# Attention's q and k kept in scratch as four rows a channel, so that one DMA of 128 rows loads an operand

## The chip, the cores and the metric

The kernel runs on one core of one Trainium2 chip. The metric is the device time of one execution in microseconds (us). The engines are PE (matrix multiply, TensorE), DVE (VectorE), ACT (ScalarE), POOL (GpSimd) and SP (SyncE, which here only issues DMAs). A profile comes from one execution, with the start and length of every instruction.

## What is computed

Two layers of a backbone over 1024 latent and 256 context tokens (T = 1280 columns, 1024 channels). A layer is: norm, one projection into four groups of heads (gated DeltaNet, Hyena, HGRN2, differential attention), an output projection, and an MLP. The part that the change touches is the differential attention, cut to what matters:

```
q = rope(rms_norm(q)); k = rope(rms_norm(k))     # 4 heads, two halves j of 32 channels
s = einsum('bqhjd,bkhjd->bhjqk', q, k) * scale
pr = softmax(s)
w = pr[:, :, 0] - lam * pr[:, :, 1]
o = einsum('bhqk,bkhe->bqhe', w, v)
```

Everything is float32. The products of q and k run on PE in the format F32R: each operand is split into a rounded part (hi) and the rest (lo), and one matmul over 128 rows adds up four products of 32 rows each. For that q stands in SBUF as the rows hi, lo, hi, lo and k as hi, hi, lo, lo, 32 rows each.

## The kernel before, in words

A layer runs in stages, each a Python generator; `mix` and `weave` interleave two of them by weights, and a scheduler of the framework then sets the order on each engine within what depends on what. Engines work through their own queue in order. SP has one queue for nearly all loads and stores: a DMA that waits, or whose descriptors find no room, holds up all that stand behind it.

The stages around the change, in `run` (L1723):

- `project` (L448) makes the projections, a unit of 128 channels at a time. What follows a unit is done in chunks of 512, 512 and 256 tokens; for q and k it is `post_d` (L637): inverse norm, rope, then `split` into the one buffer `dhl` (tag `lf`, one buffer, shared with HGRN2's `lf`). ACT copies the hi part (L254), DVE subtracts to get the lo part (L255), and SP stores both with one DMA (L657).
- `scratch` (L427) lays out the buffers in DRAM. `dq` and `dk` are `[2, 128, 2, T]`: hi or lo, channel, block of 128 channels, token. So a channel has one row of 5 KB for hi and one for lo, far apart.
- `hgrn` (L988) runs as the leading stage, and `rest()` in `run` as the filling one: the end of `project`, then the loads of attention's first head (`load` in `attn`, L1146), then `hyena` (L1441) woven with the modulation products `mods` (loads `modw`, L341; matmuls `pmod`, L363).
- `attn` (L1137) then leads, with what is left of `hyena`, `mods` and the next layer's filters as the fill. Each of its four heads needs two q tiles and two k tiles of 128 rows. The loads of the next head are issued when the third query block of a head begins (`qi == 2`).

`load` fills a tile with two DMAs, each of 64 rows. For q the source is hi and lo of 32 channels, the same both times. For k it is hi of 32 channels repeated twice, then lo repeated twice, a source with a step of zero in its outermost dimension. So a head is 8 DMAs, and both layers together have 64.

`hyena` transposes its input on PE first (`put`, L1468). The input `u` is loaded at L1455, and the filter bases (`bfl`, `bil`, `bfc`, `bic`) at L1311, gates (`xg`) at L1458. In layer 0 it runs for the context tokens first and then for the latents, in one and the same buffer `u`: the first pass stores its result (L1542) before the second pass loads. In layer 1 it runs for the latents only.

Of the kernel before, what the change touches and what calls it, by code (L numbers as in the profile page):

```python
# [9 lines left out]
F32 = mybir.dt.float32  # L10
# [11 lines left out]
T = SEQ + CTX  # L22
# [218 lines left out]
class K:  # L241
# [185 lines left out]
    def scratch(self, l):  # L427
        S = self.S = {}
        for n in CM_COL:
            if n in ("hf", "hb"):  # L430
                S["k" + n] = self.dram(f"k{n}_{l}", [128, 2, T])
                S["l" + n] = self.dram(f"l{n}_{l}", [128, T // 64, 2, 2, 64])
            elif n in ("dq", "dk"):
                S[n] = self.dram(f"{n}_{l}", [2, 128, 2, T])
            elif n[0] != "g":
                S[n] = self.dram(f"{n}_{l}", [128, 2, T])
        g = self.dram(f"g_{l}", [128, 6, T])
        S["gk"], S["gv"], S["gq"] = [g[:, 2 * j:2 * j + 2] for j in range(3)]
        for n in list(S):
            for i in range(2):  # L440
                S[n, i] = S[n][:, :, i] if n in ("lhf", "lhb", "dq", "dk") else S[n][:, i]
        S["g"] = g
        for n, a, w in TM:
            S[n] = self.dram(f"{n}_{l}", [128, NT, w])
        for k in range(KT):
            S["o", k] = self.dram(f"o{k}_{l}", [128, T])
# [190 lines left out]
    def post_d(self, l, tp, name, i, u, a, n):  # L637
        nc = self.nc
        u = u[:, a:a + n]
        r = self.inv_norm(tp, u, self.c["bones32"], 1.0 / 32, 32 * EPS)  # L640
        y = self.e(tp, 2, n)
        nw = self.P["dqw" if name == "dq" else "dkw"]
        nc.vector.scalar_tensor_tensor(y, u, nw, r, ALU.mult, ALU.mult)
        if a < SEQ:

            rc, rs = self.e(tp, 1, n), self.e(tp, 3, n)
            nc.sync.dma_start(rc, self.i["c_rcos"][:, a:a + n])
            nc.sync.dma_start(rs, self.i["c_rsin"][:, a:a + n])
            t2 = self.e(tp, 0, n)
            p = self.aux("prope")  # L650
            nc.tensor.matmul(p[:, :n], self.c["rperm"], y, start=True, stop=True)
            nc.vector.tensor_mul(t2, p[:, :n], rs)
            nc.vector.tensor_mul(y, y, rc)
            nc.vector.tensor_add(y, y, t2)
        hl = tp.tile([128, 2, 512], F32R, tag="lf", name="dhl", bufs=1)
        self.split(hl[:, 0, :n], hl[:, 1, :n], y, lo_eng=nc.vector)
        nc.sync.dma_start(self.S[name, i][:, :, a:a + n].rearrange("x p t -> p x t"), hl[:, :, :n].bitcast(F32))  # L657


    def gdn(self, l):  # L660
# [476 lines left out]
    def attn(self, l, qp):  # L1137

        nc, tc, S, P = self.nc, self.tc, self.S, self.P
# [6 lines left out]
        def load(i, b):  # L1146

            out = ops[i, b] = []
            for j in range(2):
                r = slice(64 * b + 32 * j, 64 * b + 32 * j + 32)  # L1150
                for nm, n in (("q", 128 * NQ), ("k", T)):
                    t = pools[heads.index((i, b)) % 2].tile([128, T], F32R, tag=f"{nm}{j}", name=f"{nm}{j}")[:, :n]
                    raw = t.bitcast(F32)
                    src = S["d" + nm, i]
                    for x in range(2):
                        v = src[:, r, :n] if nm == "q" else src[x:x + 1, r, :n].to_broadcast([2, 32, n])
                        nc.sync.dma_start(raw[64 * x:64 * x + 64], v)
                    out.append(t)

        pools = [qp]  # L1160
        load(*heads[0])
        yield 0
        es = ExitStack()
# [95 lines left out]
        for h, (i, b) in enumerate(heads):  # L1259
            for qi in range(NQ):  # L1260
                if qi == 2 and h + 1 < len(heads):
                    load(*heads[h + 1])
                cur = scores(i, b, qi)
                yield 0.4
                for f in ([todo] if todo else []):
                    yield from f()
                if qi == 0:
                    old, oT = oT, tp.tile([128, 64 * NT], F32, tag="oT", name="oT")

                def todo(i=i, b=b, qi=qi, cur=cur, oT=oT):  # L1270
                    w, rs = weights(*cur)
                    yield 0.2
                    pair.append((turn(w), rs))
                    yield 0.2
                    if qi % 2:
                        values(i, b, oT, qi - 1, pair)
                        pair.clear()
                        yield 0.6
                    if qi == NQ - 1:
                        norm(i, b, oT)  # L1280
# [574 lines left out]
```

## Time and profile before

| | us |
|---|---|
| median of 3 runs | 4706.38 (4696.30 to 4708.67) |
| the profiled execution | 4706.21 |
| its span, first to last instruction | 4704.4 |
| PE busy in the span | 4081.9 (87%) |
| DVE, ACT, POOL busy | 2352.6 (50%), 1620.4 (34%), 1082.8 (23%) |
| mean granted TensorE clock | 0.915 of full speed |

The profile is a page with busy times, a chain of waits and the costliest groups of instructions, and behind it a trace that can be asked: the instructions of one engine in order of time (the timeline), who waited for whom, and the busy time of the engines with the DMA traffic in a stretch. A line number is that of the code above. The time in brackets behind an instruction is how long its engine stood idle before it, and what ended that.

### The profile page before, as it was taken

What the parts mean: (1) busy time and instruction counts of PE and PEld (TensorE: products, weight loads), DVE (VectorE), ACT (ScalarE), POOL (GpSimd) and SP (SyncE); (2) the same over time, 40 slices, a digit from 0 to 9 for tenths busy, and PEclk for the clock granted to TensorE, in tenths of its full rate; (3) what the DMA queues carried; (4) which work ended last, traced back from release to release, by engine and by line L of the source; (5) the groups of instructions that cost most, each with busy time, mean ns of one, the idle gap of its engine ahead of it and who ended that gap; (6) DMA issues with size and microseconds to landing.
All of it is one profiled execution on the core that took longest, in us unless ns stands there. A gap on an engine that the chain in (4) does not pass through costs nothing. (4 is left out here: it accounts for less than half of the span.)

```text
span 4704.4 us, 81485 instructions
## 1 busy us (share of the span) xinstructions
PE 4081.9 (87%) x33270; PEld 3290.9 (70%) x33270; DVE 2352.6 (50%) x4599; ACT 1620.4 (34%) x3165; POOL 1082.8 (23%) x1101
## 2 busy tenths in 40 slices
PE   4987999867477799999999987999847788999999
PEld 2866877655355588888888776776635667888887
DVE  7566556647587353222222756456647874322222
ACT  3453413423245342212122554514313464321222
POOL 1121110000121344333333221120001114433333
PEclk7998999877789899999999998899867899999999
DMA  5236633224324421111111326634342234111112
GB/s 194 87 89 169 199 97 111 92 91 145 97 84 147 156 79 50 36 41 36 41 36 49 118 82 159 184 107 124 97 143 71 84 113 145 64 48 49 46 49 88
DMA packets 381355, 458.61 MB, mean 97 GB/s; under 512 B 137108, under 2 KB 244244, under 8 KB 378933
## 3 DMA queue, kind: packets, MB, share of 16 engines
q1 hardware_dynamic: 379156, 448.42, 30.4%
q0 software_dynamic: 1824, 4.98, 0.4%
q8 instruction: 262, 4.29, 0.4%
q14 instruction: 113, 0.92, 0.1%
HBM read 343.81 MB, written 109.48 MB: 96 GB/s over the span
## 5 line engine op out<-in xcount | busy, mean ns | idle before, releaser
L255 POOL TENSOR_TENSOR wlo<-wraw,whi 128x512 fp32r<-128x512 f32 x360 | 478.3, 1334 | 743.3 <-ACT whi L254 739.2
L254 ACT CAST whi<-wraw 128x512 fp32r<-128x512 f32 (+1 forms) x480 | 296.5, 619 | 905.4 <-PE pt L260 757.4
L1597 DVE SCALAR_TENSOR_TENSOR tx<-pt,mod,tx 128x512 f32<-128x512 f32 (+1 forms) x360 | 250.6, 696 | 590.6 <-PE pt L261 590.5
L260 PE MATMUL pt<-fl,whi 128*128 128x512 f32 (+1 forms) x1280 | 475.4, 371 | 0.0
L261 PE MATMUL pt<-fh,wlo 128*128 128x512 f32 (+1 forms) x1280 | 475.4, 371 | 0.0
L259 PE MATMUL pt<-fh,whi 128*128 128x512 f32 (+1 forms) x1280 | 475.1, 371 | 0.0
L261 PE MATMUL pt<-hh,wlo 128*128 128x512 f32 (+1 forms) x1280 | 471.2, 368 | 2.8 <-POOL wlo L255 2.8
L260 PE MATMUL pt<-hl,whi 128*128 128x512 f32 (+1 forms) x1280 | 471.9, 369 | 0.0
L259 PE MATMUL pt<-hh,whi 128*128 128x512 f32 (+1 forms) x1280 | 471.2, 368 | 0.4 <-ACT f L1630 0.4
L1631 DVE TENSOR_TENSOR f<-f 128x512 f32<-128x512 f32 (+1 forms) x160 | 149.3, 935 | 622.9 <-ACT f L1630 619.2
L259 PE MATMUL pproj<-hh,whi 128*128 128x512 f32 (+1 forms) x960 | 372.0, 387 | 7.0 <-ACT u L487 6.4
L260 PE MATMUL pproj<-hl,whi 128*128 128x512 f32 (+1 forms) x960 | 362.0, 377 | 0.0
L261 PE MATMUL pproj<-hh,wlo 128*128 128x512 f32 (+1 forms) x960 | 360.6, 376 | 0.0
L255 POOL TENSOR_TENSOR fl<-f,fh 128x512 fp32r<-128x512 f32 (+1 forms) x160 | 191.5, 1198 | 390.6 <-ACT fh L254 387.0
L260 PEld LDWEIGHTS pt<-fl,whi 128*128 128x128 f32 x1280 | 240.1, 188 | 47.3 <-issue 0.2
L261 PEld LDWEIGHTS pt<-fh,wlo 128*128 128x128 f32 x1280 | 240.1, 188 | 47.1 <-issue 0.5
L259 PEld LDWEIGHTS pt<-fh,whi 128*128 128x128 f32 x1280 | 240.1, 188 | 47.0 <-ACT whi L254 0.2
L261 PEld LDWEIGHTS pt<-hh,wlo 128*128 128x128 f32 x1280 | 241.3, 188 | 44.3 <-POOL wlo L255 4.1
L259 PEld LDWEIGHTS pt<-hh,whi 128*128 128x128 f32 x1280 | 241.3, 189 | 41.0 <-ACT f L1630 0.8
L260 PEld LDWEIGHTS pt<-hl,whi 128*128 128x128 f32 x1280 | 241.3, 189 | 40.3 <-issue 0.2
L259 PEld LDWEIGHTS pproj<-hh,whi 128*128 128x128 f32 x960 | 186.5, 194 | 47.1 <-ACT u L487 8.2
L1199 ACT ACTIVATE p<-psc,mx 128x1280 f32<-128x1280 f32 (+1 forms) x144 | 178.0, 1238 | 120.0 <-DVE mx L1198 71.1
(380 smaller groups left out, 8330.7 us busy)
## 6 DMA issues: line engine op xcount, KB each, us to landing
wraw<-mlp_w SPq DMA_DIRECT2D x296, 256.0 KB
modw<-mod_w SPq DMA_DIRECT2D x80, 512.0 KB
wraw<-w_cm SPq DMA_DIRECT2D x88, 256.0 KB
wraw<-w_out SPq DMA_DIRECT2D x64, 256.0 KB
kv<-kvd SPq DMA_DIRECT2D x40, 256.0 KB
k<-dk SPq DMA_DIRECT2D x32, 320.0 KB
bfl<-c_hyfl SPq DMA_DIRECT2D x4, 2048.0 KB
modw<-mod_w SPq DMA_DIRECT2D x4, 2048.0 KB
```

What stands on the lines that cost most here:

```text
L254: (hi_eng or nc.scalar.copy)(hi, src)
L255: (lo_eng or nc.gpsimd).tensor_tensor(lo, src, hi.bitcast(F32), ALU.subtract)
L259: nc.tensor.matmul(ps, wh, xh, start=start, stop=False)
L260: nc.tensor.matmul(ps, wh, xl, start=False, stop=False)
L261: nc.tensor.matmul(ps, wl, xh, start=False, stop=stop)
L1199: nc.scalar.activation(p[j], A, AF.Exp, bias=mx[:, j:j + 1], accum_out=sm[:, j:j + 1])
L1597: nc.vector.scalar_tensor_tensor(xm, p, G[:, m, v:v + 1], xm, ALU.mult, ALU.add)
L1631: nc.vector.tensor_mul(f, f, f)
```

## The change

`dq` and `dk` become `[2, 128, 4, T]`: block of 128 channels, channel, row, token. A channel has four rows of 5 KB that follow one another, for q hi, lo, hi, lo and for k hi, hi, lo, lo. A chunk of `post_d` is stored with two DMAs in place of one, each of hi and lo: for q into the rows 0-1 and then 2-3, for k into the rows 0 and 2 and then 1 and 3. An operand is loaded with one DMA in place of two: 32 channels by 4 rows are 128 consecutive rows in DRAM, and go to the 128 partitions. The 128 rows of a tile then stand in another order (channel by channel, not part by part), the same for q and k, so that a matmul adds up the same products in another order.

```
             elif n in ("dq", "dk"):
-                S[n] = self.dram(f"{n}_{l}", [2, 128, 2, T])
+
+                S[n] = self.dram(f"{n}_{l}", [2, 128, 4, T])
...
-                S[n, i] = S[n][:, :, i] if n in ("lhf", "lhb", "dq", "dk") else S[n][:, i]
+                S[n, i] = S[n][:, :, i] if n in ("lhf", "lhb") else S[n][i] if n in ("dq", "dk") else S[n][:, i]
...
-        nc.sync.dma_start(self.S[name, i][:, :, a:a + n].rearrange("x p t -> p x t"), hl[:, :, :n].bitcast(F32))
+        for d in range(2):
+            rows = slice(2 * d, 2 * d + 2) if name == "dq" else slice(d, 4, 2)
+            nc.sync.dma_start(self.S[name, i][:, rows, a:a + n], hl[:, :, :n].bitcast(F32))
...
-                r = slice(64 * b + 32 * j, 64 * b + 32 * j + 32)
                 for nm, n in (("q", 128 * NQ), ("k", T)):
                     t = pools[heads.index((i, b)) % 2].tile([128, T], F32R, tag=f"{nm}{j}", name=f"{nm}{j}")[:, :n]
-                    raw = t.bitcast(F32)
-                    src = S["d" + nm, i]
-                    for x in range(2):
-                        v = src[:, r, :n] if nm == "q" else src[x:x + 1, r, :n].to_broadcast([2, 32, n])
-                        nc.sync.dma_start(raw[64 * x:64 * x + 64], v)
+                    c0 = 64 * b + 32 * j
+                    nc.sync.dma_start(t.bitcast(F32), S["d" + nm, i][c0:c0 + 32, :, :n].rearrange("c r t -> (c r) t"))
                     out.append(t)
```

How instructions move. SP's queue in layer 0, where the last HGRN2 loads are followed by the first head's operands and the loads of `mods` and `hyena`; before:

```order
L1157 DMA q_11251<-dq_108 64x1x1280
L534 DMA v_113<-tm 128x512
L1157 DMA q_11251<-dq_108 64x1x1280
L1157 DMA k_11254<-dk_109 64x1x1280 x2
L1157 DMA q_11257<-dq_108 64x1x1280 x2
L1157 DMA k_11260<-dk_109 64x1x1280 x2
L341 DMA modw<-mod_w 128x1024 x2
L1446 DMA sk<-hysk 128x4
L1311 DMA bfc<-c_hyfc 128x512
L1311 DMA bic<-c_hyic 128x512
L1455 DMA u<-yv_100 128x2x256
```

and now:

```order
L1156 DMA q_11263<-dq_108 128x1280
L535 DMA v_113<-tm 128x512
L1156 DMA k_11265<-dk_109 128x1280
L1156 DMA q_11267<-dq_108 128x1280
L1156 DMA k_11269<-dk_109 128x1280
L341 DMA modw<-mod_w 128x1024 x2
L1445 DMA sk<-hysk 128x4
L1310 DMA bfc<-c_hyfc 128x512
L1310 DMA bic<-c_hyic 128x512
L1454 DMA u<-yv_100 128x2x256
```

Eight DMAs of 64 rows have become four of 128 rows, at the same place; what stands behind them is the same. The other seven heads change likewise; at three of them a load of `modw` also changes places.

PE's queue at the first transpose of `hyena` (`put`), among the HGRN2 products (`psc`, `po`, `pkv`); before:

```order
L1074 MATMUL pkd<-c_ident,X 128x128 x2
L1094 MATMUL psc<-X 32x32 x56
L1094 MATMUL psc<-q,k 32x32 x16
L1113 MATMUL po<-S_7382,X 64x128 x2
L1121 MATMUL pkv<-it,kd 64x64 x8
L1115 MATMUL po<-it,A_7379 64x64 x4
L1113 MATMUL po<-S_7383,X 64x128 x2
L1115 MATMUL po<-it,A_7379 64x64 x4
L1468 MATMUL put<-c_ident,u 128x128 x4
```

and now:

```order
L1077 MATMUL pkd<-c_ident,X 128x128 x2
L1097 MATMUL psc<-X 32x32 x42
L1467 MATMUL put<-c_ident,u 128x128 x4
L363 MATMUL pmod<-modw,cst 32x128 x8
L1097 MATMUL psc<-X 32x32 x4
```

The transposes stand some steps earlier, ahead of the end of that HGRN2 tile. In the two other places where `hyena` begins (layer 0, latents; layer 1) their neighbours are the same as before.

SP's queue at the stores of k in layer 0, where a chunk's store is followed by the rope table of the next; before:

```order
L647 DMA e_9160<-c_rcos 128x512
L657 DMA dk_109<-dhl 128x2x512
L1036 DMA k<-khb_106 128x2x128
L1041 DMA q<-hq_103 128x2x128
L648 DMA e_8587<-c_rsin 128x512
```

and now:

```order
L648 DMA e_9163<-c_rcos 128x512
L660 DMA dk_109<-dhl 256x1x512 x2
L1039 DMA k<-khb_106 128x2x128
L649 DMA e_8588<-c_rsin 128x512
L1044 DMA q<-hq_103 128x2x128
```

One store has become two, and a rope load and an HGRN2 load have changed places.

## Rows read from the trace of the kernel before

**Rows 1.** The page, part 1: busy time, share of the span, instructions.

```profile
PE 4081.9 (87%) x33270; PEld 3290.9 (70%) x33270; DVE 2352.6 (50%) x4599; ACT 1620.4 (34%) x3165; POOL 1082.8 (23%) x1101
```

**Rows 2.** PE's waits over the span, the first entry: total us, times, longest us.

```profile
PE put L1468 <- DMA u<-yv: 113.5, 3, 46.5
```

**Rows 3.** PE's timeline at the three stalls: start, length, instruction, [idle before <-releaser].

```profile
1020.22 0.63 PE L1074 MATMUL pkd<-c_ident,X 128*128 128x128 f32 x2
...
1062.32 1.13 PE L1468 MATMUL put<-c_ident,u 128*128 128x128 f32 x4 [32.60 <-DMA u<-yv]
...
1210.34 2.90 PE L1468 MATMUL put<-c_ident,u 128*128 128x128 f32 x12 [34.41 <-DMA u<-yv]
...
3485.46 1.13 PE L1468 MATMUL put<-c_ident,u 128*128 128x128 f32 x4 [46.48 <-DMA u<-yv]
```

**Rows 4.** Windows, the third stall: busy PE, PEld, DVE, ACT, POOL; PEclk, DMA share, GB/s.

```profile
3439.00:3485.40 46.40, 0.00 (x0) 0.00 (x0) 0.00 (x0) 0.61 (x2) 0.19 (x1) 0.50 0.61 187
```

**Rows 5.** SP's timeline before the first stall; the length is how long the issue took.

```profile
998.47 0.57 SPq L1157 DMA_DIRECT2D q<-dq  x1
...
1024.03 16.81 SPq L341 DMA_DIRECT2D modw<-mod_w  x2
...
1047.02 1.66 SPq L1455 DMA_DIRECT2D u<-yv  x1
```

**Rows 6.** Windows: DMA share and GB/s under q and k loads, and under others.

```profile
1085.00:1090.00 5.00, 4.45 (x68) 3.56 (x68) 3.63 (x16) 0.58 (x1) 0.00 (x0) 0.62 0.97 369
1160.00:1165.00 5.00, 4.93 (x49) 3.87 (x46) 4.56 (x7) 3.16 (x7) 0.00 (x0) 1.00 0.13 53
...
3455.00:3475.00 20.00, 0.00 (x0) 0.00 (x0) 0.00 (x0) 0.00 (x0) 0.00 (x0) 0.50 1.00 301
```

**Rows 7.** The DMA issues: tiles, queue, count, KB each (1024 bytes).

```profile
modw<-mod_w SPq DMA_DIRECT2D x80, 512.0 KB
...
k<-dk SPq DMA_DIRECT2D x32, 320.0 KB
...
dk<-dhl SPq DMA_DIRECT2D x8, 512.0 KB
...
bil<-c_hyil SPq DMA_DIRECT2D x2, 2048.0 KB
```

**Rows 8.** SP's timeline before the second stall.

```profile
1144.10 1.11 SPq L1157 DMA_DIRECT2D q<-dq  x2
...
1175.53 0.38 SPq L1542 DMA_DIRECT2D o<-u  x1
...
1203.91 0.58 SPq L1455 DMA_DIRECT2D u<-yv  x1
```

**Rows 9.** DVE's timeline: the last product of the first hyena pass.

```profile
1164.95 0.42 DVE L1540 TENSOR_TENSOR u<-u,xg 128x256 f32<-128x256 f32 x1
```

**Rows 10.** SP's timeline before the third stall.

```profile
3411.82 0.55 SPq L1157 DMA_DIRECT2D q<-dq  x1
...
3454.25 2.32 SPq L1455 DMA_DIRECT2D u<-yv  x1
```

**Rows 11.** SP's timeline in the projections of layer 0: a store of k.

```profile
835.80 0.38 SPq L657 DMA_DIRECT2D dk<-dhl  x1
```

**Rows 12.** ACT's timeline: the copies into the stored buffer.

```profile
824.47 0.62 ACT L254 CAST dhl<-e 128x512 fp32r<-128x512 f32 x1
...
834.39 0.60 ACT L254 CAST dhl<-e 128x512 fp32r<-128x512 f32 x1
...
838.86 0.42 ACT L254 CAST dhl<-e 128x256 fp32r<-128x256 f32 x1
```

**Rows 13.** PE's timeline in layer 1: a stall of the modulation products.

```profile
3648.49 1.08 PE L363 MATMUL pmod<-modw,cst 128*32 128x128 f32 x16 [7.16 <-DMA modw<-mod_w]
```

**Rows 14.** Windows: right after the second stall, and attention in layer 1.

```profile
1210.30:1220.30 10.00, 9.70 (x54) 8.30 (x55) 1.28 (x3) 4.88 (x9) 0.00 (x0) 0.55 0.14 53
...
3485.00:3880.00 395.00, 303.28 (x3289) 232.68 (x3289) 311.04 (x494) 175.39 (x330) 56.54 (x69) 0.81 0.29 97
```

## The prediction, made before the changed kernel ran

> **What bounds the kernel now.** First the page's busy times: PE is busy for 4081.9 of 4704.4 us [rows 1], so the question is where its other 622 us go. Next the list of PE's waits: the longest by far is `put`, the transpose with which `hyena` begins, for the DMA that loads its input `u`: 113.5 us in three waits [rows 2]. Then PE's timeline at the three places: idle for 32.60 us up to 1062.32 (layer 0, context tokens), 34.41 up to 1210.34 (layer 0, latents), 46.48 up to 3485.46 (layer 1) [rows 3]. In the third stall the windows show PE and DVE at 0.00, ACT at 0.61 and POOL at 0.19 us busy of 46.4 [rows 4]: nothing runs beside it, so a microsecond taken from such a wait is a microsecond of the kernel, unless something else is late next.
>
> Why `u` is late stands in SP's timeline. Before the first stall SP begins to issue the first head's q and k at 998.47 and comes to the two `modw` behind them only at 1024.03; these take another 16.81 us to issue, and `u` goes out at 1047.02 [rows 5]. An issue that finds room takes half a microsecond; these are held up. The windows say by what: while only q and k move, the DMA share is 0.13 of 16 engines, that is two engines, at 53 GB/s; with other transfers under way it is 0.97 at 369 GB/s, or 1.00 at 301 [rows 6]. The code has the two: the outermost dimension of each of these loads is hi/lo or the repeat, of size 2. At a head's 8 x 320 KB [rows 7] = 2.62 MB, 53 GB/s makes 49 us. Since SP's queue is in order and each later DMA has a share on those two engines, all of it waits for them. The same holds at the second stall (loads from 1144.10, the store behind them out at 1175.53, `u` at 1203.91) [rows 8] and the third (3411.82, `u` out at 3454.25) [rows 10].
>
> **The loads.** They become DMAs whose outermost dimension is 128 on both sides, as in `modw`, `bil` and `u` themselves. For their rate I take the nearest rows: 301 GB/s, the 20 us in which mostly `bil` and its like move; the bounds are 53 (no change) and 369 [rows 6]. For start and landing I add 1.5 us: a 512 KB store issued at 835.80 is done before the next copy into its buffer at 838.86 [rows 11, 12], 3.06 us in all, of which 0.52 MB at 301 GB/s are 1.7.
>
> First stall. Ahead of `u`, with it: 2.62 MB, two `modw` of 512 KB, `bfc`, `bic` and `u` of 256 KB each, 4.46 MB, 14.8 us at 301. From 998.5 that lands at 1014.8. PE came to `put` at 1062.3 - 32.6 = 1029.7; in the new order some 8 us sooner, since `put` now stands behind the 42 small products that follow the `pkd` of 1020.22 [rows 3], at about 1021.5. Both are later than 1014.8: **32.6 us go, 0 stay**.
>
> Second stall. Here the load of `u` must wait for the store of the first pass's result out of the same buffer. That result is complete at 1165.4 [rows 9], but SP was held by the loads until 1175.53, and the store then stood behind their data. Now the loads are done by 1144.1 + 8.7 + 1.5 = 1154. From 1166: the store, `modw`, `xg` and `u` (tiles of 1024 KB), another `modw`, 3.3 MB with the store, 11 us, landing at 1178.5. PE arrives at 1175.9. **2.5 stay, 32 go**.
>
> Third stall. Ahead of `u`: q 4 x 256 KB and k 4 x 320 KB (2.36 MB), two `modw` (1.05), `bfl` and `bil` of 2048 KB (4.19), `u` (1.05 by its tile), 8.65 MB, 28.7 us at 301, landing at 3442. PE arrives at 3439.0. **3 stay, 43 go**. At 369 GB/s nothing would stay in any of the three.
>
> The loads of the other five heads hold SP up as well, but there they run beside attention, and PE waits little for it: 7.16 us for one `modw` in layer 1 [rows 13]. Its stretch is DVE's more than PE's (DVE 311 of 395 us [rows 14]), so of 0 to 7 I take 3. [...]
>
> **The stores.** 22 chunks are stored twice, so 22 DMAs are added. SP pays 0.38 us for an issue [rows 11], 8 us in all, and saves 32 issues of loads: nothing, hidden by SP's idle time between the HGRN2 loads; without that cover it would be those 8 us. What can cost is the single buffer `dhl`: ACT's copy of the next chunk waits until both stores have landed, and behind it on ACT stand HGRN2's exponentials and the copies that empty the projections' PSUM, for which PE waits. The price of the second store lies between 0 and the whole 3.06 us of the first; I take 1.7, its data at 301 GB/s. From one chunk of 512 to the next there are 9.9 us, in which the store hides; only a 256-token chunk follows as closely as 4.5 us [rows 12], and of those there are 6. 6 x 1.7 = 10, half of it on PE's path since PE has products of its own queued: **5 us lost**, bounds 0 and 22 x 3.06 = 67. The extra 10 MB of writes run where the engines have room.
>
> **Sum.** 32.6 + 32 + 43 + 3 + 3 - 5 = 108.6 off the profiled execution's 4706.2 (which is the median to 0.2 us): 4597.6. I round up for small new waits: **4600**, own range 4582 to 4612.
>
> **Rivals.**
> (a) *Each DMA pays its start and landing in turn.* I charge them once a chain, because the transfers of the rows follow each other at a share of 1.00 [rows 6]. If all 10, 6 and 9 DMAs of the three chains pay the 1.4 us that the store shows beyond its data [rows 11, 12], `u` lands at 1027 (6 stay, by the new order), 1185.5 (10 stay) and 3453 (14 stay): 24 less is gained, **4622**. [...]
> (b) *The freed transfers collide.* Loads, bases, `modw` and HGRN2's tiles now want the engines at once. At 150 GB/s, half of what I take, `u` lands at 998.5 + 29.7 + 1.5 = 1029.7 (8 stay, by the new order), 1166 + 22 + 1.5 = 1189.5 (14 stay) and 3411.8 + 57.7 + 1.5 = 3471 (32 stay). Gain 24 + 21 + 14 = 59, with the small terms **4645**. For: over the whole third stall the rate is only 187 at a share of 0.61 [rows 4]. Against: in part of that only the two engines move.
> [...]
> (d) *Slower.* A load's time is set by its rows, one at a time, and not by the number of engines: the head's 512 rows of 5 KB then take their 49 us as before, all three stalls stay, and the doubled stores cost 1.4 to 3.06 us each on ACT's path, 31 to 67: **4740**. It decides if a head's four loads take over some 40 us. Against: `bil` and the like move at 301 to 369 [rows 6]. [...]
> (e) *No change.* The loads are fast and PE waits at the same places for something else that was hidden behind `u`: **4706**. Against: nothing else works in the stalls [rows 4].
>
> **How the numbers follow.** Forecast 0.58, (a) 0.13, (b) 0.10, (c) 0.13, (d) 0.03, (e) 0.03. The likeliest is 4600. The range takes in the forecast's own, (a), (c) as far as 4570 and most of (b): 4570 to 4650. A measurement of this kernel can tell about 0.3%, 14 us, from no change: faster 0.94, the same 0.03, slower 0.03.
>
> **What would show it.** Right: four q and k issues a head at about 0.5 us each, a DMA share near 1 right after them, `u` issued some 5 us after the first head's first load, and `put` almost gone from PE's waits (under 10 of 113.5 us). The stores: ACT's copies into `dhl` 1 to 2 us later in the short chunks, with no new entry of PE. Wrong: a share that stays at 0.13 (d); `put` still waiting 10 us or more a place, with gaps in the share (a) or a low rate at a full share (b); or PE idle there with another releaser (e).

## The result, and the profile after

The change takes 4577.17 us (median of 4 runs, 4570.20 to 4589.74), the kernel before 4704.45 in the same series: a ratio of 0.9735, 95% interval 0.9720 to 0.9751. Two later series, on two chips, gave 0.9732 (0.9717 to 0.9747) and 0.9721 (0.9700 to 0.9742). So some 125 us are gained where 106 were forecast. The profiled execution took 4573.73 us, its span is 4572.0.

The page's busy times, to be read against [rows 1]:

```profile
PE 4068.5 (89%) x33270; PEld 3281.2 (72%) x33270; DVE 2353.6 (51%) x4599; ACT 1619.7 (35%) x3165; POOL 1090.3 (24%) x1101
```

The span is 132.4 us shorter. PE's idle time fell from 4704.4 - 4081.9 = 622.5 us to 4572.0 - 4068.5 = 503.5, that is by 119.0; its busy time fell by 13.4, for the same 33270 matmuls.

Where the idle time went is in the list of PE's waits (total, times, longest), to be read against [rows 2]:

```profile
PE psc L1196 <- ACT p L1198: 73.4, 39, 10.3
...
PE psc L1097 <- issue: 32.4, 17, 5.5
...
PE pmod L363 <- DMA modw<-mod_w: 3.8, 5, 1.2
...
PE put L1467 <- ACT wT L1220: 0.5, 1, 0.5
```

Before the change three of these entries read:

```profile
PE psc L1197 <- ACT p L1199: 71.0, 42, 10.3
...
PE psc L1094 <- issue: 29.8, 18, 2.5
...
PE pmod L363 <- DMA modw<-mod_w: 10.6, 6, 7.2
```

The entry that led the list, `put` for `u` with 113.5 us, is gone; what is left of `put` are 0.5 us behind ACT. `pmod`'s wait for `modw` fell from 10.6 to 3.8, the 7.16 of [rows 13] included. No other entry took their place: first now stands attention's wait for ACT, which was 71.0 before.

SP's timeline shows why, at the first and the third place (compare [rows 5, 10]):

```profile
1004.63 0.42 SPq L1156 DMA_DIRECT2D q<-dq  x1
...
1006.57 0.32 SPq L1156 DMA_DIRECT2D k<-dk  x1
1006.98 0.41 SPq L1156 DMA_DIRECT2D q<-dq  x1
1007.48 0.44 SPq L1156 DMA_DIRECT2D k<-dk  x1
1007.97 1.30 SPq L341 DMA_DIRECT2D modw<-mod_w  x2
...
1011.75 0.52 SPq L1454 DMA_DIRECT2D u<-yv  x1
...
3337.27 0.32 SPq L1156 DMA_DIRECT2D q<-dq  x1
...
3345.24 0.52 SPq L1454 DMA_DIRECT2D u<-yv  x1
```

Nothing holds SP up at these places any more: the two `modw` go out in 1.30 us where they took 16.81, and `u` is issued 7.1 us after the first load in place of 48.6, in layer 1 after 8.0 in place of 42.4.

The windows tell at what rate (busy PE, PEld, DVE, ACT, POOL; PEclk, DMA share, GB/s), compare [rows 6]:

```profile
1006.00:1011.00 5.00, 3.52 (x183) 2.68 (x183) 1.55 (x5) 3.42 (x8) 0.39 (x1) 1.00 0.97 345
1011.00:1016.00 5.00, 0.47 (x32) 0.33 (x31) 0.23 (x2) 0.72 (x3) 0.00 (x0) 0.56 1.01 402
...
3344.00:3349.00 5.00, 4.33 (x27) 2.74 (x28) 1.87 (x7) 2.53 (x6) 0.00 (x0) 0.73 1.02 409
3349.00:3354.00 5.00, 3.22 (x211) 2.69 (x210) 2.11 (x6) 2.42 (x7) 0.19 (x1) 0.50 1.02 429
```

Where 53 GB/s flowed at a share of 0.13, it is now 345 to 429 at a share of 1. And PE's timeline at the three places where it stood in [rows 3]:

```profile
1015.26 0.47 PE L1097 MATMUL psc<-q,k 64*32 64x32 f32 x32 [5.48 <-issue]
...
1031.70 0.84 PE L1467 MATMUL put<-c_ident,u 128*128 128x128 f32 x4
...
1145.26 2.05 PE L1467 MATMUL put<-c_ident,u 128*128 128x128 f32 x12
...
3364.19 1.13 PE L1467 MATMUL put<-c_ident,u 128*128 128x128 f32 x4
```

No brackets behind the three `put`: PE goes on without a pause. (PE comes to the first of them 27.1 us after the first load, where the forecast had 23; no term hangs on that.) The first line is a new and smaller wait, spoken of at the end.

Last the granted clock, in the 10 us from each `put` on. Before the change, at the first and the third place (the second is in [rows 14]):

```profile
1062.30:1072.30 10.00, 5.83 (x92) 4.05 (x92) 5.45 (x13) 1.17 (x2) 1.78 (x1) 0.83 0.65 212
3485.40:3495.40 10.00, 9.94 (x58) 8.06 (x58) 4.76 (x17) 2.93 (x5) 0.00 (x0) 0.81 0.71 237
```

and after it, at all three:

```profile
1031.70:1041.70 10.00, 8.04 (x148) 5.90 (x142) 6.47 (x21) 2.27 (x5) 1.28 (x1) 0.98 0.60 196
1145.20:1155.20 10.00, 9.51 (x71) 8.06 (x70) 7.03 (x10) 6.96 (x12) 1.58 (x1) 1.00 0.16 56
3364.10:3374.10 10.00, 9.97 (x55) 8.30 (x55) 4.14 (x17) 3.61 (x7) 0.19 (x1) 0.69 0.78 266
```

The mean clock goes from 0.83 to 0.98 and from 0.55 to 1.00 at the first two places, and from 0.81 down to 0.69 at the third. The work before (busy time by clock) at the clock after gives an estimate of 0.9 + 4.4 - 1.7 = 3.6 us saved. That leaves some 10 us of the 13.4 by which PE's busy time fell, and these do not follow the stalls. In experiments 1 to 3 below `put` waits 5.7, 49.4 and 113.6 us for `u`, and their pages have, in that order:

```profile
PE 4082.5 (89%) x33270; PEld 3292.4 (72%) x33270; DVE 2351.8 (51%) x4599; ACT 1620.2 (35%) x3165; POOL 1080.1 (24%) x1101
PE 4071.0 (88%) x33270; PEld 3283.7 (71%) x33270; DVE 2356.7 (51%) x4599; ACT 1620.6 (35%) x3165; POOL 1085.1 (23%) x1101
PE 4078.3 (87%) x33270; PEld 3289.1 (70%) x33270; DVE 2358.2 (50%) x4599; ACT 1621.8 (34%) x3165; POOL 1085.5 (23%) x1101
```

Experiment 1 has hardly a stall left and PE is as busy as before the change, 4082.5 against 4081.9; experiment 2 has 49 us of stalls and 4071.0. Three executions of the change itself lie between 4065.0 and 4069.0. What lowers the busy time stays open.

### The profile page after: what moved, and what is told of

The parts are those of the page before. It is cut to its first block, busy times and chain, and to the rows that moved or that the text cites. A ratio compares the mean times of both kernels' runs of the same rounds, so it can differ in the third digit from the quotient of the medians.

```text
span 4572.0 us, 81465 instructions
## 1 busy us (share of the span) xinstructions
PE 4068.5 (89%) x33270; PEld 3281.2 (72%) x33270; DVE 2353.6 (51%) x4599; ACT 1619.7 (35%) x3165; POOL 1090.3 (24%) x1101
## 5 line engine op out<-in xcount | busy, mean ns | idle before, releaser
L259 PEld LDWEIGHTS pproj<-hh,whi 128*128 128x128 f32 x960 | 186.2, 194 | 49.4 <-issue 9.6
```

The source lines that it names most:

```text
L259: nc.tensor.matmul(ps, wh, xh, start=start, stop=False)
```

## The experiments

The theory (A): how many of the 16 DMA engines a load works on was the whole matter, and in this kernel that went with its outermost size: at size 2, before, the share is 0.13, that is two engines [rows 6], at 128, now, 0.97 to 1.02 (windows above), that is all sixteen. Its rivals: that there are fewer DMAs, that a channel's rows stand side by side, or that each DMA pays a start and a landing of its own. All times are medians; the ratio is to the kernel before on the same chip.

| experiment | us | ratio, 95% interval | put's waits for `u`, us |
|---|---|---|---|
| 1 four DMAs, old layout | 4588.63 | 0.9750 (0.9731 to 0.9768) | 5.7 |
| 2 one DMA, 4 engines | 4626.07 | 0.9835 (0.9819 to 0.9851) | 49.4 |
| 3 doubled stores, 2 engines | 4712.70 | 1.0014 (1.0003 to 1.0025) | 113.6 |
| 4 loads on POOL's queue | 4610.21 | 0.9797 (0.9776 to 0.9818) | 26.4 |
| 5 four DMAs, rows apart | 4589.03 | 0.9764 (0.9746 to 0.9782) | 3.6 |
| 6 four DMAs, rows adjacent | 4594.83 | 0.9771 (0.9754 to 0.9789) | 4.2 |
| 7 two rows, single store | 4588.25 | 0.9749 (0.9733 to 0.9765) | 0.7 |
| 8 the change again | 4578.76 | 0.9732 (0.9717 to 0.9747) | 0.5 |
| 9 four DMAs, all partitions | 4596.45 | 0.9768 (0.9747 to 0.9789) | 7.1 |
| 10 single store, all partitions | 4571.59 | 0.9720 (0.9700 to 0.9741) | 0.3 |
| 11 the change, third time | 4571.01 | 0.9721 (0.9700 to 0.9742) | 0 |
| 12 the middle half in one DMA | 4590.23 | 0.9754 (0.9729 to 0.9779) | 3.7 |

**1. Sixteen engines without the new layout.** The kernel before, with its scratch and its single store; only the load is cut otherwise.

```
-                    for x in range(2):
-                        v = src[:, r, :n] if nm == "q" else src[x:x + 1, r, :n].to_broadcast([2, 32, n])
-                        nc.sync.dma_start(raw[64 * x:64 * x + 64], v)
+                    for x in range(4):
+                        nc.sync.dma_start(raw[32 * x:32 * x + 32], src[x % 2 if nm == "q" else x // 2, r, :n])
```

> Layout and single store as before; each operand is loaded with four DMAs of 32 rows (16 a head where the change has 4, and before 8). Theory A (a load's speed is the number of DMA engines that its outermost sizes allow; 2 before, 16 here and in the change): the three waits of put fall from 113.5 us to under 10, the DMA share right behind the loads is near 1, and the time is 4565 to 4585, since the stores are not doubled. Rival B (what counts is fewer DMAs, or that the source rows follow each other in DRAM): with 16 DMAs a head and rows far apart the waits stay or grow, 4700 or more. Rival C (each DMA pays a start and a landing of some 1.4 us in turn): 16 a head cost about 17 us a head more than in the change, of which only the three places count: 4577 + 30 to 50 = 4607 to 4627.

Measured 4588.63, 117 us faster than before. The loads' number doubled in place of halving, and the rows stand as far apart as ever; so neither makes the gain, and B falls. C falls as well, at 4607 to 4627. The share right behind the loads is near 1, as A has it:

```profile
1004.00:1016.00 12.00, 5.06 (x185) 3.58 (x183) 7.22 (x25) 4.65 (x12) 0.39 (x1) 0.77 1.02 244
```

A's main claim holds, but 4588.63 is some 4 us over its upper end; what that is, the later experiments ask.

**2. One DMA with four engines.** The change, but the source walked part by part.

```
-    ... S["d" + nm, i][c0:c0 + 32, :, :n].rearrange("c r t -> (c r) t"))
+    ... S["d" + nm, i][c0:c0 + 32, :, :n].rearrange("c r t -> r c t"))
```

> Layout, stores and the number of loads as in the change (one DMA of 128 rows an operand), but the source is walked part by part, so that the outermost size is 4 in place of 32 channels' 128 rows. Theory A (engines by outermost size): 4 engines at twice the 53 GB/s of two, so a head takes 22 to 25 us; beside the chains ahead of u put waits some 3 us at the first place, 0 to 5 at the second, 10 to 15 at the third, and the time is 4577 + 13 to 23 = 4590 to 4600. Rival B (one DMA in place of two is what counts): as the change, 4577, put under 2 us.

The windows during the loads, and PE's timeline at the three places:

```profile
1004.00:1016.00 12.00, 5.78 (x202) 4.65 (x203) 7.22 (x25) 3.83 (x11) 0.39 (x1) 0.69 0.27 98
```

```profile
1039.98 1.13 PE L1467 MATMUL put<-c_ident,u 128*128 128x128 f32 x4 [15.52 <-DMA u<-yv]
...
1161.95 2.90 PE L1467 MATMUL put<-c_ident,u 128*128 128x128 f32 x12 [9.37 <-DMA u<-yv]
...
3409.95 1.13 PE L1467 MATMUL put<-c_ident,u 128*128 128x128 f32 x4 [24.51 <-DMA u<-yv]
```

The same layout, the same bytes and one DMA an operand, and 49 us of the stalls are back: a share of 0.27 and 98 GB/s, four engines' worth, nearly twice the 53 of two. B is out. A's direction and rate are right, its size isn't: 4626 against 4590 to 4600. I had let the transfers behind the loads go out at once. In the trace SP is held up again: the two `modw` take 12.50 us to issue, and `u` goes out 23.7 us after the first load.

```profile
1000.45 0.60 SPq L1156 DMA_DIRECT2D q<-dq  x1
...
1004.59 12.50 SPq L341 DMA_DIRECT2D modw<-mod_w  x2
...
1024.15 2.09 SPq L1454 DMA_DIRECT2D u<-yv  x1
```

Both the held queue and the bytes ahead of `u` count, and the rows tell how much of PE's wait falls before and after the issue of `u`. In the kernel before it is 17.3, 28.0 and 15.3 us before the issue, 60.6 of 113.5, and 52.9 after it [rows 3, 5, 8, 10]. Here PE comes to the first `put` at 1039.98 - 15.52 = 1024.46, when `u` has just gone out, so that all of this wait falls after the issue.

How the hold-up works can be read from the packets (one row of q or k each, by the packet records of the trace). At the second place of the kernel before, the last four loads take 6.0 to 6.3 us each to issue, and during each the two engines finish 62 or 63 such rows, about one load of 64. So SP gets rid of one load for each that is done; 221 to 227 rows are then still unfinished. The first three loads there went out in 0.49 to 0.53 us each, the fourth in 5.13. That the loads behind have a share on the two engines is read from the first place: of the 256 rows of 4 KB of the two `modw`, 224 have ended by 1044.2, and the other 32, two sixteenths, end from 1056.3 to 1059.7, about when the last row of q and k ends (1057.2) and after it.

**3. The stores alone.** Layout and doubled stores of the change, loads cut into two DMAs with an outermost size of 2.

```
+                    for x in range(2):
+                        v = S["d" + nm, i][c0:c0 + 32, 2 * x:2 * x + 2, :n].rearrange("c r t -> r c t")
+                        nc.sync.dma_start(t.bitcast(F32)[64 * x:64 * x + 64], v)
```

> Layout and doubled stores as in the change, loads as two DMAs of 64 rows whose outermost size is 2, as before. Theory A: the loads are as slow as before, put's waits return with about 113 us, and the difference to the kernel before is the price of the doubled stores alone: the prediction's 5 us gives 4709, free stores 4704, its bound of 67 gives 4771. Rival B (four rows of a channel side by side make the loads fast): put under 30 us, 4580 to 4620.

PE's waits and a window during the loads:

```profile
PE put L1469 <- DMA u<-yv: 113.6, 3, 50.8
```

```profile
1013.00:1035.00 22.00, 14.82 (x314) 10.69 (x313) 11.33 (x40) 4.59 (x12) 0.19 (x1) 0.61 0.13 54
```

With two engines the share is 0.13 at 54 GB/s again and `put` waits 113.6 us, though the rows now stand side by side. B is out. The ratio of 1.0014 (1.0003 to 1.0025) prices the doubled stores: 6.6 us, between 1.4 and 11.8. It is the price of all that differs from the kernel before, the layout included.

**4. The loads on another queue.** The kernel before, `nc.sync` changed to `nc.gpsimd` in `load`.

> The kernel before with the loads of q and k issued from POOL's queue in place of SP's, still two engines each. Theory A1 (u is late because SP's queue is in order and held up by the loads, so that u isn't even issued): u is issued within 10 us of the first load, put's waits mostly go, and the time is 4590 to 4615. Theory A2 (u is late because its own share on the two busy engines waits for their 49 us of data): u is issued early but lands late, put's waits stay above 60 us, and the time is 4650 to 4710.

```profile
1010.00:1030.00 20.00, 0.91 (x33) 0.52 (x33) 5.58 (x20) 0.51 (x2) 0.00 (x0) 0.50 1.09 143
```

Inconclusive. The time is A1's, 4610, and `u` is issued at 1009.94, but A1's first condition isn't met: that is 13.1 us after the first load, not 10. `put` still waits 18.35 us at the first place and 8.0 at the third, and the window shows that the premise is wrong: the DMA share is 1.09, so from POOL's queue these loads do not stay on two engines. The first head's 512 packets of 5 KB take 527 ns on average and all start within 34.2 us, so that some 512 x 0.527 / 34.2 = 8 engines work on them; in the kernel before it is 223 ns and 57.1 us, 2 engines. So this run can't tell the held queue from the two engines' backlog.

**What the cutting costs.** In experiment 1 the 5 KB packets took 332 ns on average in the first head's loads, in the change 224. Six experiments ask why. Of the second head's 512 such packets:

| loads | mean ns | up to 210 ns | from first to last start, us |
|---|---|---|---|
| the change (first, second, third series) | 215, 210, 213 | 93%, 94%, 93% | 7.1, 7.1, 7.3 |
| 1: 32 rows, far apart, into 32 partitions | 342 | 8% | 12.4 |
| 5: 32 rows, 20 KB apart, into 32 partitions | 356 | 6% | 12.4 |
| 6: 32 adjacent rows, into 32 partitions | 338 | 10% | 11.9 |
| 7: 64 rows, into 64 partitions | 359 | 7% | 12.4 |
| 9: 32 rows, into every fourth partition | 267 | 54% | 11.2 |
| 10: q 128 rows; k 64, into every second partition | 221 | 85% | 7.6 |
| 12: 32, 64 and 32 adjacent rows | 312 | 20% | 11.4 |

**5 and 6. Rows apart, rows adjacent.** Both are the change with four DMAs of 32 rows an operand; in 5 each takes one part of all 32 channels, in 6 the 32 consecutive rows of 8 channels.

```
+                        nc.sync.dma_start(t.bitcast(F32)[32 * x:32 * x + 32], S["d" + nm, i][c0:c0 + 32, x, :n])
```

```
+                        v = S["d" + nm, i][c0 + 8 * x:c0 + 8 * x + 8, :, :n].rearrange("c r t -> (c r) t")
+                        nc.sync.dma_start(t.bitcast(F32)[32 * x:32 * x + 32], v)
```

> Layout and doubled stores as in the change; each operand is loaded with four DMAs of 32 rows, one part of all 32 channels each, so that the rows of a DMA stand 20 KB apart in DRAM and no row is read twice. In the first experiment a packet of 5 KB took 330 to 340 ns, in the change 222. Theory Q (rows apart are read slower than rows that follow each other): 330 ns here, and the time is that of the first experiment and its unsaved stores, 4590 to 4600. Theory P (a DMA of 32 rows fills only 32 of the 128 partitions, and that is what slows it): 330 ns here too. Theory R (the first experiment read each row twice, shortly after each other): 222 ns here, 4577 to 4585.

> As the experiment before this one, but each of the four DMAs takes the 32 consecutive rows of 8 channels, into 32 partitions. Theory Q (rows apart): 222 ns a packet of 5 KB and the time of the change, 4570 to 4585. Theory P (32 partitions): 330 ns, 4590 to 4600. Theory R (rows read twice): 222 ns, as Q. If four DMAs cost by their number alone, the packets take 222 ns and the time is still 4590 or more.

In both the packets are slow and the time is 10 to 16 us over the change's. So Q (distance in DRAM) and R (rows read twice) fall; P stands, and so does the rival that few rows a DMA for each engine make slow packets. The slow packets show in the rate at a full share, in 6 and then in the change of the same series:

```profile
1002.00:1016.00 14.00, 6.29 (x227) 4.72 (x225) 7.22 (x25) 5.61 (x14) 0.39 (x1) 0.77 0.98 236
```

```profile
1006.50:1016.00 9.50, 4.37 (x199) 3.39 (x202) 1.63 (x5) 4.51 (x11) 0.39 (x1) 0.92 1.00 373
```

**7. Two rows a channel, stored once.** Meant to beat both: k's repeat moved inside, behind the channels, two DMAs an operand.

```
+                        v = S["d" + nm, i][c0:c0 + 32, :, :n].rearrange("c r t -> (c r) t") if nm == "q" else S["d" + nm, i][c0:c0 + 32, x:x + 1, :n].to_broadcast([32, 2, n])
+                        nc.sync.dma_start(t.bitcast(F32)[64 * x:64 * x + 64], v)
```

> A version meant to be better than both: two rows a channel (hi, lo, side by side), stored once as in the kernel before, and an operand loaded with two DMAs of 64 rows with the channels outermost (q: 64 consecutive rows, twice; k: hi of 32 channels, each repeated, then lo). 16 engines, and no doubled store. The price of the doubled stores came out as 7 us (1 to 12) in the third experiment, so with loads as fast as the change's the time is 4577 - 7 = 4570 (4560 to 4578). Theory R (rows read twice are slow) and theory P (64 partitions): packets over 250 ns, and 4575 to 4590.

4588.25: as P and R had it, the packets are slow and the time is 9.5 us over the change's beside it, though the store is saved. With it ran the change again:

> The change once more, on the chip of these runs, for comparison: 4577 (4565 to 4590), packets of 5 KB at 222 ns, under 2 us of put's waits.

It came out at 4578.76, as expected.

**9 and 10. All partitions in every DMA.** 9 is 5 with `t.bitcast(F32)[x::4]` in place of the 32 neighbours. 10 is 7 with q in one DMA (each row twice) and k's two in every second partition, `t.bitcast(F32)[x::2]`; 11 is the change beside them.

> Layout and doubled stores as in the change; four DMAs of 32 rows an operand as in the experiment with rows apart (one part of all 32 channels each, 20 KB apart in DRAM), but each fills every fourth of the 128 partitions in place of 32 neighbours. Theory P (the span of partitions that one DMA fills sets how long a packet takes): 5 KB in 210 to 225 ns, put's waits under 2 us, 4572 to 4584. Theory N (the number of DMAs, or how few rows each gives an engine, sets it): 330 to 350 ns as with 32 neighbours, put 3 to 6 us, 4586 to 4598.

> A second try at a version better than both: two rows a channel (hi, lo), stored once; q with one DMA of 128 rows (each row twice), k with two DMAs of 64 rows, each into every second partition, so that each spans all 128. Theory P: packets of 5 KB at 210 to 230 ns, put under 2 us, and without the doubled stores 4566 to 4578. Theory N: k's packets, half of all, at 330 ns, 4578 to 4590. If reading a row twice is what costs, q's are slow as well, and the time is 4585 to 4595.

> The change once more on the chip of these two runs: 4577 (4565 to 4590).

9 lies between the theories: 267 ns, over half of the packets at the change's speed and 27% over 320; its time is N's, 4596. It differs from 5 only in the partitions that a DMA fills, and the packets go from 356 to 267 ns: so the partitions do matter for the packets. But the time does not follow, a ratio of 0.9768 against 0.9764. That the slow packets are what costs the time is therefore not shown; the number of DMAs is a rival that stands. 10 is as P had it, 221 ns at the second head (237 at the first) and 4571.59. It stores half as much as the change and equals it, 4571.59 against 4571.01 beside it; a gain of the 6.6 us that the stores cost isn't shown.

**12. The middle half.** The change with three DMAs an operand, for the partitions 0 to 31, 32 to 95 and 96 to 127.

> Layout and doubled stores as in the change; an operand is loaded with three DMAs of adjacent rows, for the partitions 0 to 31, 32 to 95 and 96 to 127. So far 90% of the change's 5 KB packets took under 210 ns, but with DMAs of 64 rows into partitions 0 to 63 or 64 to 127 only 1 to 13%, and with 32 neighbours 10 to 15%; the rest took up to twice as long. Theory N (few rows a DMA for each engine make slow packets): the 64 rows for 32 to 95 are as slow as those for 0 to 63, at most 20% of the packets under 210 ns, and the time is 4586 to 4598. [...]

At the three places 20 to 29% of the packets are under 210 ns, more than N's 20 at two of them (over all eight heads it is 1 to 38%); the time, 4590.23, lies in N's 4586 to 4598. It settles nothing: why a narrower DMA makes slower packets stays open between the partitions that are filled together and the few rows that each engine gets.

The price of the cutting is not in PE's idle time, 510.4 us in 6 and 509.6 in the change of its series, but in its busy time, 4080.0 against 4069.0. Over all runs the busy time goes the same way: where q comes in one DMA a tile (the change three times, experiments 2 and 10) PE is busy for 4059.0 to 4071.0 us, in all others and before the change for 4076.4 to 4088.5. The mean granted clock of the profiled executions is 0.929 to 0.931 in the change and 0.932 in experiment 10, 0.924 to 0.927 in 1, 5, 6, 7, 9 and 12; but it is 0.923 in 2, with 49 us of stalls and a busy time of 4071.0. That the cut loads cause the lower clock is an inference, each figure but the change's is from one execution, and no run moved the clock alone.

## Why the prediction was right, and where it was short

The direction, the mechanism and the range were right: 4577 lies in 4570 to 4650, though outside the forecast's own 4582 to 4612. Point by point:

- **What bounds the kernel.** Right. The wait for `u` came from loads on two engines: 53 to 54 GB/s with two (before, and experiment 3), 98 with four (2), 345 to 429 with sixteen (other loads are among these). The DMA share went with the outermost size of the loads: 0.13 of 16 engines at size 2, 0.27 at 4, and about 1 at 32 (1.02, experiment 1) and at 128 (0.97 to 1.02, the change).
- **The three stalls**, 107.6 of 113.5 us to go: all of it went. The 5.5 that were to stay rested on 301 GB/s; 345 to 429 was measured.
- **`modw`**, 3 of 0 to 7: the total of that wait fell by 6.8, the upper end.
- **The clock**, the second 3 in the sum, for a higher granted clock after the stalls: it was the author's estimate, and no run shows the term. What the runs showed in its place: in the 10 us from each `put` on the mean clock went from 0.83 to 0.98, from 0.55 to 1.00 and, at the third place, from 0.81 down to 0.69, an estimate of 3.6 us by the busy times there. What the sum lacked is another 10 us of shorter busy time that does not go with the stalls (experiments 1 and 2) and whose cause stays open.
- **The stores**, 5 us of 0 to 67: 6.6 (1.4 to 11.8) by experiment 3 agrees, though experiment 10, with half the stores, is no faster than the change. ACT's timeline shows the place (compare [rows 12]):

```profile
827.01 0.62 ACT L254 CAST dhl<-e 128x512 fp32r<-128x512 f32 x1
837.27 0.60 ACT L254 CAST dhl<-e 128x512 fp32r<-128x512 f32 x1
843.80 0.41 ACT L254 CAST dhl<-e 128x256 fp32r<-128x256 f32 x1
```

  From one chunk to the short one behind it there are 6.53 us where there were 4.47; between the long ones 10.26 where there were 9.92. That is the 1 to 2 us in short chunks that was named, with no new entry among PE's long waits; where on PE's path the price falls isn't shown.
- **The sum.** 108.6 became 132.4 in the profiled executions: 113.0 from `put`, 6.8 from `modw`, 13.4 from PE's busy time, less 2.6 of the longer wait for "issue", and 1.8 net over all other entries. Of the 24 us beyond the forecast's sum, some 5 were stalls that were to stay, 4 `modw`, 10 the busy time, and 5 the stores, which the forecast took off on top. The price of the stores is already inside these differences.
- **The rivals.** (a) asked for gaps and 4622: the share is 0.97 to 1.02 in the four windows above, and experiment 1 with four times the DMAs still has 4589. (b) asked for 150 GB/s. (d) asked for loads of over 40 us a head: `u`, behind them, was used 27 us after the first load, and the stores cost 7 us, not 31 to 67. (e) asked for another releaser at `put`: none. The time lies on the side of (c), for which the range goes down to 4570: the rate was 345 to 429 GB/s where the forecast took 301, `modw`'s wait fell by 6.8 where it took 3, and the busy time by 13.4, mostly not after the stalls; free stores lie outside experiment 3's 1.4 to 11.8, though only just.

## What to carry to other kernels

When an engine waits for a small transfer, read the issuing queue's timeline: a single issue that takes 4 to 15 us in place of 0.5 is held up by what stands ahead of it, and the DMA share there tells how many engines that uses. A row that counts two issues can also hold a wait between them: after the change two `modw` at 1067.97 make a row of 12.57 us, of which 11.8 are SP's wait for PE's `pmod` (the list of SP's waits from 1060 to 1085 has `SPq L341 <- PE pmod L363: 14.4, 2, 11.8`). A zero-step repeat or a pair of parts outermost in a load that SP issues confined it to as many engines here (a share of 0.13 of 16 at 53 GB/s), and with 128 consecutive rows outermost the share was 0.97 to 1.02 and the queue behind it free (the two `modw` out in 1.30 us, not 16.81), here 2.7% of the kernel. Load a 128-row tile with one DMA: cut into narrower ones on the same engines it gave some 10 to 25 us of this back (not in experiment 10, where q is whole and k's two DMAs span all partitions).

## What the runs showed that was not expected

One of PE's waits grew. Before the change:

```profile
1005.45 0.36 PE L1094 MATMUL psc<-q,k 64*32 64x32 f32 x32 [1.83 <-issue]
```

The `psc` that waited 1.83 us for "issue" here waits 5.48 after the change, at a share of 1.01 and 402 GB/s, with hardly any work on the other engines; over the span that entry grew by 2.6 us. In the other two executions of the change it is 4.87 and 4.62, with the loads on POOL's queue 6.46, but 3.48 in experiment 6 and 1.96 in 9, so that a full share alone does not make it. The packet records show what these waits go with. In the change's trace each of the 12 `psc` waits for "issue" of over 1.5 us ends 1.1 to 1.5 us after a 16 KB packet of the kind "instruction" has ended, and so do the 13 before. Here that packet starts 3.0 us after the wait began; before, it had started already when the wait began. That PE waits there for its own instructions, and that the loads make them late, is an inference.

The mean time of a 5 KB row at the second head ran from 210 to 359 ns by how the tile was cut into DMAs, and to 427 from POOL's queue.
